# Order of the last two product stages of a block inverse, and of a modulation matmul, in a two-layer diffusion-transformer kernel

## The chip, the cores and the metric

The kernel runs on one core of a Trainium2 chip. The metric is the device time of one execution in microseconds; lower is better. The core has a matmul engine (TensorE, "PE" in the profile, its weight loads "PEld"), VectorE ("DVE"), ScalarE ("ACT"), GpSimd ("POOL"), and a queue of DMA issues ("SP").

## The reference, cut to what matters

One step of a two-layer trunk is computed for 512 latent and 128 context tokens of width 2048. Two pieces of it are touched.

Every layer starts with an RMSNorm that is modulated by a vector computed from the condition:

```python
def adaln(cond, w, b):
    m = (jax.nn.silu(cond) @ w + b)[:, None, :]
    return jnp.split(m, 3, axis=-1)
hp = rmsnorm(xp, norm_g[layer]) * (1.0 + scale_p) + shift_p
```

Layer 1 is a recurrence over tokens, once in each direction, for 32 heads of size 64:

```python
def step(s, inp):
    r_t, w_t, k_t, v_t, kk_t, a_t = inp
    sa = jnp.einsum('bhij,bhj->bhi', s, -kk_t)
    s = s * w_t[:, :, None, :] + sa[..., None] * (kk_t * a_t)[:, :, None, :] + v_t[..., None] * k_t[:, :, None, :]
    return s, jnp.einsum('bhij,bhj->bhi', s, r_t)
```

The kernel does this recurrence in chunks of 64 tokens. In a chunk each step reads what the earlier steps of the chunk wrote, which is a triangular system of 64 x 64 for each head. Its inverse is what the function below builds.

## The kernel before, in words

**The start (lines 244 to 304).** The modulation of layer 0 is a product of a 2048-vector (two of them, padded to 32 columns) with a matrix of 2048 x 6144, of which eight blocks of 512 columns are done here. `adaln` takes one block: for each of 16 slices of the 2048 it loads a tile `araw` of 128 x 512 floats (256 KB, pool `xt0`, eight buffers) and multiplies (line 176). The four column tiles of the array, 32 columns wide, are used in turn (`tile_position=(0, j)`), and their four partial sums are added at the end, after a copy to SBUF (`row`, line 180) and four transposes (line 183). Four rounds `b` of the loop at line 291 do two blocks each. In rounds 1 to 3 the generator is advanced by the numbers in `JW` between six projection jobs of the round before (`part` and `first`, 24 matmuls at line 126 each), and after the blocks `modulate` makes the inputs of the next jobs. A projection loads a tile `raw`, ScalarE makes its rounded part `whi` (line 100), GpSimd the remainder `wlo` (line 101), and three products are added up. All DMAs are issued in order from the SP queue.

**The recurrence (layer 1).** It has 32 units, of a pair of heads and a half of the tokens of both directions. `unit(n)` writes PE's instructions by hand (`manual_schedule`): the steps of the recurrence of unit `n` (`stage_c`), between them steps of `fill`, which put projection matmuls of line 126 there, and then the table `P2`, which prepares the next units: `inv` is `stage_inv`, `bk` transposes (`pbk`, copied to `BKn` by ScalarE), `pre` transposes (`pvt`, copied to `UV`) and products (`pmv`), `bonus` a sum (`pbn`), `a2` Gram products (`gram`, which VectorE masks into `GG`). The other engines' order is made by a scheduler from the program's order and priorities.

`stage_inv` has four stages of 32 x 32 products, all written into one PSUM tile `CC`. The two directions `z` have partitions 0 to 63 and 64 to 127; in each, the 64 x 64 system is split into two blocks of 32, and there are ten systems `q`.

- Stage 1 (L1243) and stage 2 (L1252) go over `q` outside and the four diagonal tiles of the array inside, 40 products each.
- VectorE then transposes the upper blocks (L1257) and ScalarE copies all four blocks of the result to `xd` (L1259).
- Stage 3 (L1265) multiplies by the off-diagonal block of the system, all ten products of the first direction on one tile of the array, (0, 32), then all ten of the second on another, (64, 96). It overwrites the lower blocks in PSUM. ScalarE copies the result (L1268, named `DD`).
- Stage 4 (L1272) does the same on the tiles (32, 0) and (96, 64), and overwrites the upper blocks. ScalarE copies with a minus sign (L1275).

A 32-bit float product is run by the engine as two passes, so 40 products show as 80 records, and 20 as 40.

Of the kernel before, what the change touches and what calls it, by code (L numbers as in the profile page):

```python
# [14 lines left out]
AF = mybir.ActivationFunctionType  # L15
# [6 lines left out]
KT = 16  # L22
# [31 lines left out]
def kernel(  # L54
# [5 lines left out]
    act, dve, pool, pe = nc.scalar, nc.vector, nc.gpsimd, nc.tensor  # L60
# [42 lines left out]
    def sigmoid(out, in_, tmp, scale=-1.0, bias=None, out_scale=-1.0):  # L103
        if bias is None:
            act.activation(out=tmp, in_=in_, func=AF.Exp, scale=scale)
        else:
            act.activation(out=tmp, in_=in_, func=AF.Exp, scale=scale, bias=bias)
        act.activation(out=tmp, in_=tmp, func=AF.Ln, bias=one_b[0:tmp.shape[0]])
        act.activation(out=out, in_=tmp, func=AF.Exp, scale=out_scale)
# [20 lines left out]
    def chunk(g):  # L130
        for end in g:
            if end:
                break

    def project(*args):
        for _ in project_steps(*args):
            pass
# [28 lines left out]
    def ada_raw(layer, n, k, sb, bufs):  # L166
        raw = sb.tile([128, 512], F32, tag="araw", name="araw", bufs=bufs)
        dma(out=raw, in_=mod_w[layer, n, :, k, :])
        return raw

    def adaln(layer, psp, tag, sb, sc, blocks, bufs):
        for n in blocks:
            ps = psp.tile([128, 512], F32, tag=tag, name="ada")
            for k in range(KT):
                j = 32 * (k % 4)
                pe.matmul(ps[j:j + 32, :], sc[:, k, :], ada_raw(layer, n, k, sb, bufs), start=(k < 4),
                          stop=(k >= 12), tile_position=(0, j))
                yield
            row = sb.tile([128, T], F32, tag="tmp", name="row")[:, 0:512]
            act.activation(out=row, in_=ps, func=AF.Copy)  # L180
            pt = psp.tile([128, 512], F32, tag=tag, name="adat")
            for j in range(4):
                pe.transpose(pt[:, j * 128:(j + 1) * 128], row[:, j * 128:(j + 1) * 128], ident)
            ada_end(layer, n, pt.rearrange("p (j g r) -> p j r g", j=4, g=4)[:, :, 0:2, :], 4)
# [57 lines left out]
    pm = l0.enter_context(tc.tile_pool(name="pm", bufs=2, space=PSUM))  # L242

    with tc.tile_pool(name="x0", bufs=1, side="right") as xp0, \
            tc.tile_pool(name="x0t", bufs=2, side="right") as xt0:
        cond = xp0.tile([128, KT, 2], F32, name="cond")
        dma(out=cond, in_=condT)
        sct = xp0.tile([128, KT, 2], F32, name="sct")
        sigmoid(sct, cond, sct)
        dve.tensor_tensor(out=scs, in0=sct, in1=cond, op=ALU.mult)  # L250
        sc = xp0.tile([128, KT, 32], F32, name="sc")
        dve.memset(sc, 0.0)
        dve.tensor_copy(out=sc[:, :, 0:2], in_=scs)
        x0 = xp0.tile([128, KT, T], F32, name="x0")
        pt = pj.tile([128, 1024], F32, tag="pj", name="ss")
        pss = [pt[:, 512 - HT:512], pt[:, 512:512 + HT]]
        for k in range(KT):
            dma(out=x0[:, k, :], in_=xT[k])
            sq = xt0.tile([128, T], F32, tag=("tmp", "hm")[k % 2], name="sq")
            act.activation(out=sq, in_=x0[:, k, :], func=AF.Square)  # L260
            if k % 2:
                dve.tensor_tensor(out=sq, in0=sq, in1=sqe, op=ALU.add)
                for p, (a, b) in zip(pss, HALVES):
                    pe.matmul(p[:, 0:HT], ones, sq[:, a:b], start=(k == 1), stop=(k == KT - 1))
            sqe = sq
        rs0 = xp0.tile([128, T], F32, name="rs0")
        rstd(rs0, pss, 1.0 / 2048, eps_b)
        for k in range(KT):
            dve.tensor_tensor(out=x0[:, k, :], in0=x0[:, k, :], in1=rs0, op=ALU.mult)
        first = [pj.tile([128, 1024], F32, tag="pj", name="first") for _ in range(2)]  # L270
        fg = [project_steps([p[:, 512 - HT:512], p[:, 512:512 + HT]], w_l0[24 + j], KT, 128, h0hi, h0lo, HALVES, 4)
              for j, p in enumerate(first)]

        def half(g):
            for _ in range(6):
                next(g)

        def part(j, b, out):
            p = pS.tile([128, 1024], F32, tag="S", name="part")
            ks = slice(4 * b, 4 * b + 4)  # L280
            project([p[:, 512 - HT:512], p[:, 512:512 + HT]], w_l0[26 + j][:, ks, :], 4, 128,
                    h0hi[:, ks, :], h0lo[:, ks, :], HALVES, 4)
            X, acc = p[:, 512 - HT:512 + HT], accs[j][:, 0:T]
            with tc.high_priority(offset=1500):
                if b == 0:
                    dve.tensor_copy(out=acc, in_=X)
                else:
                    dve.tensor_tensor(out=acc if out is None else out, in0=acc, in1=X, op=ALU.add)

        JOBS, JW = (0, 4, 1, 5, 2, 3), (None, (5, 5, 5, 5, 5, 5), (5, 5, 5, 5, 5, 5), (5, 6, 7, 8, 6, 0))  # L290
        for b in range(4):
            ga = adaln(0, pm, "pm", xt0, sc, (b, 4 + b), 8)
            if b:
                for i, job in enumerate(JOBS):
                    for _ in range(JW[b][i]):
                        next(ga, None)
                    if job < 4:
                        part(job, b - 1, None)
                    else:
                        chunk(fg[job - 4])  # L300
            for _ in ga:
                pass
            for k in range(4 * b, 4 * b + 4):
                modulate(x0[:, k, :], 0, k, h0hi, h0lo, xt0)
        lp = xp0.tile([128, 256], F32, name="lp")
        dma(out=lp, in_=vec[:, NVEC - 256:NVEC])
        lamt = xp0.tile([128, 132], F32, name="lamt")
        dve.tensor_tensor(out=lamt[:, 0:64], in0=lp[:, 0:64], in1=lp[:, 64:128], op=ALU.mult)
        dve.tensor_tensor(out=lamt[:, 64:128], in0=lp[:, 128:192], in1=lp[:, 192:256], op=ALU.mult)
        dve.tensor_reduce(out=lamt[:, 128:130], in_=lamt[:, 0:128].rearrange("p (a b) -> p a b", a=2),  # L310
                          axis=AX.X, op=ALU.add)
        act.activation(out=lamt[:, 128:130], in_=lamt[:, 128:130], func=AF.Exp)
        dve.tensor_tensor(out=lamt[:, 130:131], in0=lamt[:, 129:130], in1=lamt[:, 128:129], op=ALU.subtract)
        nlam = cst.tile([128, 1], F32, name="nlam")
        dve.tensor_scalar(out=nlam, in0=lamt[:, 130:131], scalar1=-LAM_INIT, scalar2=None, op0=ALU.add)
# [522 lines left out]
    with ExitStack() as l1:  # L838
# [32 lines left out]
        for t in Xds:  # L871
            dma(out=t.rearrange("p c -> (p c)").rearrange("(p c) -> p c", p=128),
                in_=xds[0][:, 0:5, :].rearrange("p q t -> p (q t)"))
# [349 lines left out]
        def stage_inv(i, u):  # L1223
            un = units[(i, u)]
            zh = halves_of(u)
            G = un.GAq
            xd = un.xd = xds[u]
            Dn, D = un.DD[:, 0], un.DD[:, 1]
            grp = [(64 * z + 32 * m, 32 * m, 2 * ca) for z, _, _, ca, _ in zh for m in range(2)]
# [5 lines left out]
            def pa(o):  # L1235
                return PA[o:o + 32].rearrange("p b (q t) -> p b q t", t=32)

            def b2(t):
                return t.rearrange("p (b q) t -> p b q t", b=2)
# [10 lines left out]
            for q in range(10):  # L1250
                for o, col, q0 in grp:
                    pe.matmul(blk(o, q), t16[o:o + 32, q, :], D[o:o + 32, q, :],  # L1252
                              start=True, stop=True, tile_position=(o, o))
            xn = un.DD[:, 0]
            for o, col, q0 in grp:
                if col == 0:
                    dve.transpose(out=b2(xn[o:o + 32]), in_=pa(o))  # L1257
            for o, col, q0 in grp:
                act.activation(out=b2(xd[o:o + 32, :, col:col + 32]), in_=pa(o), func=AF.Copy)  # L1259
            yield  # L1260
            t32 = xn
            for z, a, b, ca, cb in zh:
                o = 64 * z
                for q in range(10):
                    pe.matmul(blk(o + 32, q), G[o:o + 32, 2 * ca + q, 32:64], xn[o:o + 32, q, :],  # L1265
                              start=True, stop=True, tile_position=(o, o + 32))
            for o in (0, 64):
                act.activation(out=b2(t32[o + 32:o + 64]), in_=pa(o + 32), func=AF.Copy)  # L1268
            yield
            for o in (0, 64):  # L1270
                for q in range(10):
                    pe.matmul(blk(o, q), t32[o + 32:o + 64, q, :], xd[o + 32:o + 64, q, 32:64],  # L1272
                              start=True, stop=True, tile_position=(o + 32, o))
            for o in (0, 64):
# [418 lines left out]
```

## Time and profile before

| what | value |
|---|---|
| median of 3 runs | 3726.73 us (3720.97 to 3733.14) |
| the profiled execution's own time | 3717.45 us |
| its span, first to last instruction | 3715.7 us |
| PE busy | 3491.8 us, 94% of the span |
| DVE, ACT, POOL busy | 59%, 43%, 32% |
| mean granted clock of PE | 0.98 |

The span covers all but 1.75 us of the execution's own time. Busy time of PE is the time in which a matmul is under way; matmuls overlap, so a busy engine need not be at its best rate.

### The profile page before, as it was taken

Reading aid. Unit: us, or ns where it says so; the run is one execution under the profiler, and the core shown is the slowest. Engines: PE = TensorE matmul, PEld = TensorE weight load, DVE = VectorE, ACT = ScalarE, POOL = GpSimd, SP = SyncE. Lnnn points to the kernel's source line nnn. Section 1 sums busy time; section 2 is a strip of 40 time slices with the busy share of each in tenths; the row PEclk is TensorE's granted clock in tenths of the full one; section 3 lists DMA queues with packets and bytes.
Section 4 is the critical chain, followed back from the end, with each engine's and each line's share of the span. In section 5 each row is a group of like instructions: output and inputs, shape, how many; then the busy total and the mean of one; then the engine's idle time right before and its main releaser. Section 6 shows DMA issues by size and latency. Waiting matters only on the chain. (4 is left out here: it accounts for less than half of the span.)

```text
span 3715.7 us, 83258 instructions
## 1 busy us (share of the span) xinstructions
PE 3491.8 (94%) x34176; PEld 3054.6 (82%) x34176; DVE 2183.1 (59%) x4232; ACT 1608.9 (43%) x3310; POOL 1189.5 (32%) x1094
## 2 busy tenths in 40 slices
PE   7999999999999989999999999999999999999998
PEld 3788889988888889887777787878878878787898
DVE  3355655666667564556666566666666666666402
ACT  2344443444444422544454444444444545445322
POOL 1222112222223344432333332323323333332444
PEclk9999999999999989999999999999999999999999
DMA  8723433333333464322222222222232222223534
GB/s 288 240 80 93 126 100 113 108 102 108 107 108 118 144 204 152 104 77 62 73 62 68 59 65 73 62 65 62 63 76 67 61 67 67 65 68 89 162 101 142
DMA packets 388462, 376.18 MB, mean 101 GB/s; under 512 B 200496, under 2 KB 242416, under 8 KB 388080
## 3 DMA queue, kind: packets, MB, share of 16 engines
q1 hardware_dynamic: 388080, 370.86, 34.3%
q8 instruction: 268, 4.39, 0.5%
q14 instruction: 114, 0.93, 0.1%
HBM read 328.51 MB, written 42.24 MB: 100 GB/s over the span
## 5 line engine op out<-in xcount | busy, mean ns | idle before, releaser
L101 POOL TENSOR_TENSOR wlo<-raw,whi 128x512 fp32r<-128x512 f32 (+1 forms) x628 | 854.4, 1361 | 2032.1 <-PE pj L126 1232.3
L126 PE MATMUL pj<-h0hi,wlo 128*128 128x320 f32 x4448 | 1091.2, 324 | 17.5 <-POOL wlo L101 17.3
L126 PE MATMUL pj<-h0hi,whi 128*128 128x320 f32 x4448 | 1089.2, 324 | 4.8 <-DVE gt L951 3.1
L126 PE MATMUL pj<-h0lo,whi 128*128 128x320 f32 x4448 | 1081.2, 322 | 1.1 <-POOL h0lo L101 0.8
L126 PEld LDWEIGHTS pj<-h0hi,wlo 128*128 128x128 f32 x4448 | 749.6, 192 | 51.9 <-POOL wlo L101 20.7
L126 PEld LDWEIGHTS pj<-h0hi,whi 128*128 128x128 f32 x4448 | 749.2, 192 | 38.3 <-issue 9.1
L126 PEld LDWEIGHTS pj<-h0lo,whi 128*128 128x128 f32 x4448 | 751.8, 191 | 29.2 <-issue 8.0
L100 ACT ACTIVATE whi<-raw 128x512 fp32r<-128x512 f32 (+1 forms) x628 | 390.5, 623 | 734.6 <-PE pj L126 444.0
L198 DVE SCALAR_TENSOR_TENSOR aacc<-araw,scs,aacc 128x512 f32<-128x512 f32 x480 | 401.7, 885 | 20.0 <-DMA araw<-in_dram 19.0
L362 DVE TENSOR_REDUCE nm<-S 128x1 f32<-128x768 f32 (+1 forms) x120 | 98.5, 821 | 257.6 <-PE S L374 257.5
L722 DVE SCALAR_TENSOR_TENSOR x<-pj,mod,xr 128x512 f32<-128x512 f32 (+2 forms) x68 | 33.3, 526 | 251.8 <-PE pj L126 246.1
L365 ACT ACTIVATE P<-S,nm 128x768 f32<-128x768 f32 (+1 forms) x120 | 95.2, 793 | 164.8 <-DVE nm L362 164.3
L1118 DVE TENSOR_TENSOR GG<-gram,con 128x512 f32<-128x512 f32 (+1 forms) x192 | 107.8, 597 | 79.6 <-PE gram L1114 79.5
L1303 ACT ACTIVATE Yn<-CC 128x128 f32<-128x128 f32 x160 | 44.4, 277 | 217.2 <-DVE rhs L1333 209.1
L1114 PE MATMUL gram<-AR,BK 64*128 64x128 f32 x1280 | 115.9, 295 | 20.8 <-DVE GG L1118 13.8
L1114 PEld LDWEIGHTS gram<-AR,BK 64*128 64x128 f32 x1280 | 91.8, 191 | 46.3 <-DVE GG L1118 24.1
L1348 DVE COPY UV<-CC 64x128 f32<-64x128 f32 x160 | 47.1, 295 | 130.6 <-ACT UV L1347 129.2
L1054 PE MATMUL plo<-lr,lw 96*128 96x320 f32 x256 | 104.1, 489 | 6.9 <-DMA lr<-lorad 6.6
L1347 ACT ACTIVATE UV<-CC 64x128 f32<-64x128 f32 x160 | 43.2, 270 | 148.0 <-PE CC L1345 147.4
L564 PE MATMUL po<-PT,vt 128*128 128x128 f32 x800 | 103.2, 276 | 0.1
L564 PEld LDWEIGHTS po<-PT,vt 128*128 128x128 f32 x800 | 98.0, 191 | 4.2 <-issue 2.5
L1056 ACT ACTIVATE tmp<-plo,vecs 128x320 f32<-128x320 f32 x128 | 67.5, 527 | 67.2 <-PE plo L1054 67.2
(338 smaller groups left out, 5306.3 us busy)
## 6 DMA issues: line engine op xcount, KB each, us to landing
raw<-in_dram SPq DMA_DIRECT2D x612, 256.0 KB
araw<-in_dram SPq DMA_DIRECT2D x384, 256.0 KB
lr<-lorad SPq DMA_DIRECT2D x128, 120.0 KB
Ld<-GG SPq DMA_DIRECT2D x64, 160.0 KB
lw<-in_dram SPq DMA_DIRECT2D x128, 48.0 KB
x<-in_dram SPq DMA_DIRECT2D x16, 320.0 KB
xr<-in_dram SPq DMA_DIRECT2D x16, 320.0 KB
DD<-Xd SPq DMA_DIRECT2D x32, 160.0 KB
```

The costliest lines, as they stand in the source:

```text
L100: act.activation(out=hi, in_=src, func=AF.Copy)
L101: (lo_eng or pool).tensor_tensor(out=lo, in0=src, in1=rf(hi), op=ALU.subtract)
L126: pe.matmul(p[:n, 0:b - a], w, x[:, kk ^ flip, a:b], start=(kk == order[0] and i == 0), stop=(kk == order[-1] + kc - 1 and i == 2))
L198: dve.scalar_tensor_tensor(out=acc[:, s], in0=raw, scalar=scs[:, k, s:s + 1], in1=acc[:, s], op0=ALU.mult, op1=ALU.add)
L362: dve.tensor_reduce(out=nm, in_=S[:, 0:nk], axis=AX.X, op=ALU.max, negate=True)
L365: act.activation(out=P[:, 0:nk], in_=S[:, 0:nk], func=AF.Exp, bias=nm, accum_out=l)
L564: pe.matmul(po[:, 0:128], H.vt[:, kt, :], PT[:, j, :], start=(j == 0), stop=(j == n - 1))
L1054: pe.matmul(ps[:, 0:HT], lw, lo, start=True, stop=True)
L1056: act.activation(out=hv(tmp, z, ca, cb), in_=c3(ps[:, 0:HT]), func=AF.Exp, scale=-1.0, bias=nw0[:, bcol:bcol + 1])
L1114: pe.matmul(ps[:, j * 128:(j + 1) * 128], BK[hs, c + j, :, :].rearrange("p a t -> p (a t)"), AR[hs, c + j, :, :].rearrange("p a t -> p (a ...
L1118: dve.tensor_tensor(out=GG[:, c:c + n, h, :], in0=ps[:, 0:n * 128].rearrange("p (j t) -> p j t", t=128), in1=maskg.rearrange("p (o t) -> p ...
L1348: dve.tensor_copy(out=UV[64:128, cgs[1], :], in_=pu[1][64:128])
```

## The change

In `adaln` the four loads of a round of the four column tiles are issued first, then its four products, and the generator stops once a round instead of once a product. It also stops after the copy `row`, so that other work stands before the transposes. `JW` counts in these new steps, and the pool has twelve `araw` buffers. In `stage_inv` stages 3 and 4 go over `q` outside and the two directions inside, so that two tiles of the array take turns. Of the four copies to `xd` only the two of the lower blocks, which stage 3 overwrites, stand ahead of stage 3, and each is written between the transposes; the two of the upper blocks are issued after stage 3's own copies, ahead of stage 4, which overwrites them.

```diff
     def adaln(layer, psp, tag, sb, sc, blocks, bufs):
...
-            for k in range(KT):
-                j = 32 * (k % 4)
-                pe.matmul(ps[j:j + 32, :], sc[:, k, :], ada_raw(layer, n, k, sb, bufs), start=(k < 4),
-                          stop=(k >= 12), tile_position=(0, j))
+            for g in range(0, KT, 4):
+                raws = [ada_raw(layer, n, g + j, sb, bufs) for j in range(4)]
+                for j, raw in enumerate(raws):
+                    pe.matmul(ps[32 * j:32 * j + 32, :], sc[:, g + j, :], raw, start=(g == 0),
+                              stop=(g == KT - 4), tile_position=(0, 32 * j))
                 yield
             row = sb.tile([128, T], F32, tag="tmp", name="row")[:, 0:512]
             act.activation(out=row, in_=ps, func=AF.Copy)
+            yield
...
-        JOBS, JW = (0, 4, 1, 5, 2, 3), (None, (5, 5, 5, 5, 5, 5), (5, 5, 5, 5, 5, 5), (5, 6, 7, 8, 6, 0))
+        JOBS, JW = (0, 4, 1, 5, 2, 3), (None, (2, 1, 2, 2, 1, 2), (2, 1, 2, 2, 1, 2), (2, 2, 1, 2, 3, 0))
         for b in range(4):
-            ga = adaln(0, pm, "pm", xt0, sc, (b, 4 + b), 8)
+            ga = adaln(0, pm, "pm", xt0, sc, (b, 4 + b), 12)
...
             for o, col, q0 in grp:
                 if col == 0:
                     dve.transpose(out=b2(xn[o:o + 32]), in_=pa(o))
-            for o, col, q0 in grp:
-                act.activation(out=b2(xd[o:o + 32, :, col:col + 32]), in_=pa(o), func=AF.Copy)
+                else:
+                    act.activation(out=b2(xd[o:o + 32, :, col:col + 32]), in_=pa(o), func=AF.Copy)
             yield
             t32 = xn
-            for z, a, b, ca, cb in zh:
-                o = 64 * z
-                for q in range(10):
+            for q in range(10):
+                for z, a, b, ca, cb in zh:
+                    o = 64 * z
                     pe.matmul(blk(o + 32, q), G[o:o + 32, 2 * ca + q, 32:64], xn[o:o + 32, q, :],
                               start=True, stop=True, tile_position=(o, o + 32))
             for o in (0, 64):
                 act.activation(out=b2(t32[o + 32:o + 64]), in_=pa(o + 32), func=AF.Copy)
+            for o in (0, 64):
+                act.activation(out=b2(xd[o:o + 32, :, 0:32]), in_=pa(o), func=AF.Copy)
             yield
-            for o in (0, 64):
-                for q in range(10):
+            for q in range(10):
+                for o in (0, 64):
                     pe.matmul(blk(o, q), t32[o + 32:o + 64, q, :], xd[o + 32:o + 64, q, 32:64],
                               start=True, stop=True, tile_position=(o + 32, o))
```

**ScalarE around stages 3 and 4 of the tenth unit, before.** `xd` are the copies of the blocks, `BKn` and `UV` copies for the steps `bk` and `pre`, `DD` the copies of stage 3's result, `whi` the rounding of a projection weight, `hl` a split for `bonus`.

```order
1495 L1259 ACTIVATE xd_14636<-CC 32x10x32 x4
1496 L1183 ACTIVATE BKn<-pbk 128x512
1497 L1205 ACTIVATE UV<-pvt 64x512 x2
1498 L1268 ACTIVATE DD<-CC 32x320 x2
1499 L100 ACTIVATE whi<-raw 128x512
1500 L100 ACTIVATE hl<-kzs 128x320
1501 L1183 ACTIVATE BKn<-pbk 128x256
1502 L1275 ACTIVATE xd_14636<-CC 32x10x32 x2
```

The same place now, where four more lines in the file have moved the numbers (L1261 and L1272 are the copies to `xd`, L1270 is stage 3's result):

```order
1511 L1261 ACTIVATE xd_14636<-CC 32x10x32
1512 L1185 ACTIVATE BKn<-pbk 128x512
1513 L1261 ACTIVATE xd_14636<-CC 32x10x32
1514 L1207 ACTIVATE UV<-pvt 64x512 x2
1515 L100 ACTIVATE whi<-raw 128x512
1516 L1270 ACTIVATE DD<-CC 32x320 x2
1517 L1272 ACTIVATE xd_14636<-CC 32x10x32 x2
1518 L100 ACTIVATE hl<-kzs 128x320
1519 L1185 ACTIVATE BKn<-pbk 128x256
1520 L1279 ACTIVATE xd_14636<-CC 32x10x32 x2
```

Two copies have left the place ahead of `UV`; two stand behind `DD`, and `whi` has moved from behind the `DD` copies to ahead of them. The `whi` has moved so in 12 of the 32 units, and in four others another ScalarE operation has (`gt` or `sqk`). By the semaphores, the second transposition of VectorE now waits for the first of the two copies, and the second copy for that transposition; before, the four copies waited for both transpositions.

**PE in round 1 of the start, before:** the products of the modulation (`ada`) between the jobs, whose own rows are left out but for the first.

```order
8 L176 MATMUL ada<-araw,sc 32x512 x8
9 L126 MATMUL part<-h0hi,whi 128x320 x2
...
21 L176 MATMUL ada<-araw,sc 32x512 x2
...
34 L176 MATMUL ada<-araw,sc 32x512 x5
...
47 L176 MATMUL ada<-araw,sc 32x512
...
51 L183 MATMUL adat<-con,row 128x128 x4
52 L176 MATMUL ada<-araw,sc 32x512 x4
```

And now (line 177 is the product, 185 the transposition):

```order
8 L177 MATMUL ada<-araw,sc 32x512 x8
9 L126 MATMUL part<-h0hi,whi 128x320 x2
...
21 L177 MATMUL ada<-araw,sc 32x512 x4
...
34 L177 MATMUL ada<-araw,sc 32x512 x4
...
47 L185 MATMUL adat<-con,row 128x128 x4
48 L177 MATMUL ada<-araw,sc 32x512 x8
```

Runs of 2, 5 and 1 have become runs of 4 and 4. Over rounds 1 to 3 the 96 products stand in 24 runs before and in 21 now. With four products to a turn of the four column tiles, and a new turn for what is over, the runs make up 36 turns before (12, 11 and 13 by round) and 30 now (8, 11 and 11); in rounds 2 and 3 the scheduler still breaks some turns up (9, 1, 2, 1 and 3 products in round 2).

## Rows read from the trace of the kernel before

**Rows 1.** The page's first part: busy time, share of the span, instructions.

```profile
PE 3491.8 (94%) x34176; PEld 3054.6 (82%) x34176; DVE 2183.1 (59%) x4232; ACT 1608.9 (43%) x3310; POOL 1189.5 (32%) x1094
```

**Rows 2.** Windows: stretch, length, busy us of engines, granted clock, DMA share, GB/s.

```profile
14.00:22.00 8.00, 7.24 (x21) 3.94 (x20) 4.01 (x5) 6.07 (x9) 0.00 (x0) 1.00 1.04 394
22.00:56.00 34.00, 26.62 (x93) 6.01 (x92) 16.02 (x30) 6.89 (x12) 0.00 (x0) 1.00 0.89 302
56.00:162.00 106.00, 102.88 (x608) 69.16 (x608) 21.74 (x45) 26.70 (x45) 27.96 (x22) 1.00 0.77 259
1640.00:3430.00 1790.00, 1678.92 (x22608) 1429.38 (x22608) 1160.39 (x2643) 853.59 (x1880) 567.07 (x630) 0.98 0.26 67
```

**Rows 3.** PE's groups by line, 1640 to 3430 us: busy, mean ns, idle before.

```profile
L1114 PE MATMUL gram<-AR,BK 64*128 64x128 f32 x1240 | 112.9, 295 | 19.5 <-DVE GG L1118 13.8 <-ACT MV L1220 3.6 <-DVE BK L1097 0.6
...
L1272 PE MATMUL CC<-xd,DD 32*32 32x32 f32 x1280 | 46.0, 197 | 0.0
L1265 PE MATMUL CC<-DD,GG 32*32 32x32 f32 x1280 | 44.1, 194 | 27.5 <-ACT xd L1259 27.2
L1252 PE MATMUL CC<-DD,t 32*32 32x32 f32 x2560 | 29.6, 194 | 2.0 <-issue 1.3 <-DVE t L1246 0.4
```

**Rows 4.** Timeline of PE in one unit: start, length us, instructions, idle before.

```profile
2384.95 0.89 PE L1252 MATMUL CC<-DD,t 32*32 32x32 f32 x80
...
2390.45 1.35 PE L1265 MATMUL CC<-DD,GG 32*32 32x32 f32 x40 [1.19 <-ACT xd L1259]
...
2394.18 1.35 PE L1272 MATMUL CC<-xd,DD 32*32 32x32 f32 x40
```

**Rows 5.** Timeline of PE: products of 64 columns on two and on four tiles.

```profile
2413.23 0.45 PE L1345 MATMUL CC<-rhs,xd 64*64 64x64 f32 x8
...
2416.09 0.34 PE L1299 MATMUL CC<-S,AR 64*64 64x64 f32 x8
```

**Rows 6.** Timeline of VectorE in the unit of rows 4.

```profile
2387.50 1.05 DVE L1257 STREAM_TRANSPOSE DD<-CC 32x320 f32<-32x320 f32 x2
2393.19 0.49 DVE L1426 TENSOR_TENSOR vT<-vT,pbn 128x320 f32<-128x320 f32 x1 [4.64 <-PE pbn L1015]
```

**Rows 7.** Timeline of ScalarE in the same unit.

```profile
2388.65 1.75 ACT L1259 ACTIVATE xd<-CC 32x320 f32<-32x320 f32 x4 [3.30 <-DVE DD L1257]
2390.42 0.60 ACT L1183 ACTIVATE BKn<-pbk 128x512 f32<-128x512 f32 x1
2391.04 1.20 ACT L1205 ACTIVATE UV<-pvt 64x512 f32<-64x512 f32 x2
2392.26 0.87 ACT L1268 ACTIVATE DD<-CC 32x320 f32<-32x320 f32 x2
...
2393.59 0.62 ACT L100 ACTIVATE whi<-raw 128x512 fp32r<-128x512 f32 x1
```

**Rows 8.** Waits of the whole span: us in total, times, longest us.

```profile
ACT whi L100 <- PE pj L126: 444.0, 246, 7.4
...
PE CC L1265 <- ACT xd L1259: 27.2, 25, 2.6
```

**Rows 9.** PE's modulation products, 14 to 165 us, by line.

```profile
L176 PE MATMUL ada<-araw,sc 128*32 128x512 f32 x256 | 60.5, 603 | 5.6 <-DMA araw<-in_dram 5.6
```

**Rows 10.** Timeline of PE in round 1 of the start.

```profile
61.41 1.05 PE L176 MATMUL ada<-araw,sc 128*32 128x512 f32 x4
62.39 0.56 PE L126 MATMUL first<-h0hi,whi 128*128 128x320 f32 x2
...
66.10 1.90 PE L176 MATMUL ada<-araw,sc 128*32 128x512 f32 x10
67.94 0.56 PE L126 MATMUL part<-h0hi,whi 128*128 128x320 f32 x2
```

## The prediction, made before the result was known

> **What bounds the kernel now.** I read the page's first part, then windows, then PE's groups by line in the stretch of the recurrence, and last timelines of single places.
>
> PE is busy for 94% of the span and no other engine for more than 59% [rows 1]. In the recurrence, 1640 to 3430 us, it is busy for 1679 of 1790 us, and its clock is granted at 0.98; the DMA engines are used for a quarter [rows 2]. PE's order is fixed there, so its own time and its waits add up, and what is taken off either shortens the stretch unless another engine then makes PE wait at a later place.
>
> The last two stages of the inverse are the odd lines in PE's groups. Stage 2 runs 2560 records in 29.6 us busy; stages 3 and 4 run half as many each in 44.1 and 46.0 us [rows 3]. In one unit that is 0.89 us for 80 records against 1.35 us for 40 [rows 4]. A record lasts about 0.19 us in all three [rows 3], so the difference is the distance between starts: (0.89 - 0.19)/79 = 9 ns where four tiles take turns, (1.35 - 0.19)/39 = 30 ns where one tile is used ten products long. Besides, PE stood idle for 27.5 us ahead of stage 3, of which 27.2 us, in 25 waits, ended with the copies to `xd` [rows 3, 8].
>
> The start is bound differently. From 14 to 22 us the DMA engines move 394 GB/s, from 22 to 56 us 302 GB/s at a share of 0.89, with PE waiting in between; from 56 to 162 us PE is busy for 102.9 of 106 us and the DMA share is 0.77 [rows 2]. There PE is the bound, and the modulation products are part of its time: 60.5 us for 128 products up to 165 us [rows 9].
>
> **The change, part by part.**
>
> *Two tiles in turn.* With four tiles, stage 2 does 80 records as 20 turns of four, (0.89 - 0.19)/20 = 35 ns a turn [rows 4]. One tile does a record in 30 ns. A turn thus costs the same whether one or four tiles are in it, and with two tiles stages 3 and 4 have 20 turns too, so they should last as long as stage 2. The only two-tile case of the trace agrees: products of 64 columns take 0.45 us for 8 records on two tiles and 0.34 us on four [rows 5], where one tile, at twice the 30 ns for twice the columns, would take some 7 x 0.06 + 0.22 = 0.64 us. The gain is 44.1 + 46.0 - 2 x 29.6 = **30.9 us** [rows 3]. Its bounds are 0, if pairs don't overlap, and 39 us, if a turn of two takes one tile's 30 ns: 20 x 0.03 + 0.19 = 0.79 us a stage, 90.1 - 64 x 0.79. A tile can't go faster than it does alone.
>
> The Trainium skill speaks against this. "TensorEngine Tiling (Array Packing)", section Performance Considerations, Instruction Overhead, says that every matmul carries about 60 cycles of overhead, so that a narrow one costs as much as one of 60 columns. Read as a cost in series, that is an estimate of 25 ns a record at 2.4 GHz, 40 records would take 1.0 us however they are ordered, and the gain would be nearly nothing. The trace does not agree with that reading: stage 2's records start 9 ns apart [rows 4].
>
> *The wait ahead of stage 3.* Before, two transpositions (1.05 us) and four copies (1.75 us) run one after the other, and stage 3 starts 0.05 us behind the last copy [rows 4, 6, 7]: 2.9 us from the first transposition. Now a transposition, a copy, the second transposition and the second copy alternate, since each waits for the one ahead: 2 x 0.52 + 2 x 0.43 and four gaps of some 0.07 are 2.2 us, 0.7 us less. The copy `BKn` (0.60 us) that now stands between the two copies fits beside the second transposition. At most 25 x 0.7 = 17.5 us of the 27.2 us come back; the least is 0, where the scheduler puts longer work between the two copies, as it does in some units. Waits average 27.2/25 = 1.1 us, but many are shorter than 0.7. I take **10 us**.
>
> *The wait ahead of stage 4.* The two copies that were taken away now stand behind stage 3's copies, and stage 4 must wait for them. In the unit shown, stage 3 ends at 2391.80, ScalarE is done with `UV` at 2392.24 and with stage 3's copies at 2393.13, and stage 4 starts at 2394.18 [rows 4, 7]: a margin of 1.05 us. Two more copies take 0.87 of it. Where `whi` (0.62 us [rows 7]) now stands ahead too, the margin is 0.44 us short, and PE comes 0.48 us earlier by its shorter stage 3; ScalarE in turn has 0.87 us less to do before. Behind a stage 4 that waits, PE's whole queue waits. The least is 0; the most, 0.8 us in each of 32 units, is 26 us. The 12 units with `whi` ahead at 0.6 us, the others near nothing, make some **8 us** lost.
>
> *What is late next.* The Gram products wait 19.5 us, 13.8 of them for VectorE's `GG` [rows 3]. VectorE's long work on the next unit is released by a PE step between stages 3 and 4 (`pbn`; it sat idle 4.6 us until then [rows 6]). What stage 3 saves moves that release too, but what stage 4 saves, (46.0 - 29.6)/32 = 0.5 us a unit [rows 3], does not: where VectorE is already the later one, PE gets to `gram` earlier and waits longer. I count about 14 units so: **7 us** given back, between 0 and all 16 us of stage 4's gain.
>
> *The start.* A run of two products (4 records) holds PE for 62.39 - 61.41 = 0.98 us, a run of five for 67.94 - 66.10 = 1.84 us [rows 10]: the first turn 0.98, each further 0.86 us. Rounds 1 to 3 had 24 runs with 36 turns, now 21 with 30: 24 x 0.98 + 12 x 0.86 less 21 x 0.98 + 9 x 0.86 is **5.5 us**. In round 0 the order of PE is unchanged and the loads set the pace. Twelve buffers allow four more loads under way; if that lifted 302 to 394 GB/s for 34 us, it would give 34 x (1 - 302/394) = 8 us; if the engines are as good as full at their share of 0.89 [rows 2], nothing. I take **3 us**, nearer to the second. Each projection weight now stands behind four or eight modulation loads in SP's queue instead of three to six, up to 2 MB, which the DMA share of 0.77 after 56 us covers; without that cover a job would start some 2 us late.
>
> *Sum.* 30.9 + 10 - 8 - 7 + 5.5 + 3 = 34.4 us. The profiled execution took 3717.45 us, 9.3 us under the median of the runs; from it the sum gives 3683, from the median 3692.3. I forecast **3692 us** for the median.
>
> **The rivals.**
>
> *More comes through.* ScalarE's copies stay in stage 4's cover, VectorE keeps up, the loads speed up: 30.9 + 17.5 + 5.5 + 8 = 62 us, 3665 us. For it: PE is the bound nearly everywhere. Against it: rows 3 show VectorE late already.
>
> *ScalarE becomes the bound.* Stage 4 waits in every unit: 30.9 + 10 - 26 - 7 + 5.5 = 13 us, 3713 us. For it: a margin of 1.05 us that loses 0.87. The Trainium skill, "TensorEngine Tiling (Array Packing)", PSUM Bottleneck, has it that tiling speeds up the products but not the copies out of PSUM, and that these then bind; by the rows here they bind only in part.
>
> *Turns don't pay.* The pairs don't overlap: 10 - 8 + 5.5 + 3, 10 us, 3716 us. Against it: rows 4 and 5.
>
> *Slower.* A `whi` waits for PE to release its buffer, up to 7.4 us at a time [rows 8]. Now 12 of them stand ahead of the copies that stage 4 waits for. If PE's releasing matmul stands just ahead of stage 4, or GpSimd frees the raw tile late, ScalarE blocks and PE with it. It decides from (34.4 + 8)/12 = 3.5 us a unit; at 7.4 us the kernel takes 3727 - 42 + 89 = 3774 us. Against it: in the unit shown and its like no idle time stands before that `whi` [rows 7].
>
> **Chances.** The forecast (20 to 48 us gained) 0.66, more 0.12, ScalarE bound 0.12, no overlap 0.06, slower 0.04. A measurement of this kernel can tell about 0.3%, 11 us, from no change. Of the ScalarE case two thirds, of the no-overlap case a third lie beyond that: faster 0.66 + 0.12 + 0.08 + 0.02 = 0.88, same 0.08, slower 0.04. The range of eight in ten goes from 3669 (most of the better case left out) to 3714 (ScalarE's case in).
>
> **What would show it.** Stages 3 and 4 at 0.85 to 0.9 us for 40 records; PE's idle time ahead of stage 3 at 15 to 20 us; a new wait ahead of stage 4 of 4 to 12 us, in the units with `whi` ahead; the idle time before `gram` up by 5 to 10 us; the last transposition of the start 5 to 12 us earlier. I am wrong if the stages stay above 1.2 us, or if the new waits on ScalarE and VectorE together exceed 30 us.

## The result, and the profile after

The changed kernel takes 3666.8 us (median of four, 3659.3 to 3670.2) against 3727.7 us for the kernel before beside it: a ratio of 0.985, with an interval of 0.983 to 0.987. By the medians that is 61 us faster, by the ratio 55, where 3692 us (35 us faster) were forecast. Timed again on another occasion the ratio was 0.987 (0.985 to 0.989), 50 us. The profiled execution took 3666.4 us, its span is 3664.6 us: 51.1 us under the span of before.

The page's first part of the changed kernel, against [rows 1]:

```profile
PE 3443.2 (94%) x34176; PEld 3014.7 (82%) x34176; DVE 2190.1 (60%) x4232; ACT 1608.0 (44%) x3310; POOL 1192.0 (33%) x1094
```

PE has 48.6 us less busy time with the same 34,176 instructions, and its weight loads 39.9 us less; the other engines differ by 7 us at most. In sum the gain is in how fast PE's instructions run, hardly in how long it waits. Its groups by line in the recurrence of the changed kernel, 1623 to 3377 us, against [rows 3] (L1267 is stage 3, L1276 stage 4, L1254 stage 2):

```profile
L1116 PE MATMUL gram<-AR,BK 64*128 64x128 f32 x1240 | 117.5, 301 | 24.8 <-DVE GG L1120 14.6 <-ACT MV L1222 8.4 <-DVE BK L1099 0.6
...
L1254 PE MATMUL CC<-DD,t 32*32 32x32 f32 x2560 | 29.7, 194 | 2.0 <-issue 1.4 <-DVE t L1248 0.4
...
L1276 PE MATMUL CC<-xd,DD 32*32 32x32 f32 x1280 | 26.7, 194 | 5.5 <-ACT xd L1272 5.4
L1267 PE MATMUL CC<-DD,GG 32*32 32x32 f32 x1280 | 26.3, 192 | 16.1 <-ACT xd L1261 15.7
```

Stages 3 and 4 fell from 44.1 and 46.0 us to 26.3 and 26.7. The wait ahead of stage 3 fell from 27.5 to 16.1 us, a new one of 5.5 us stands ahead of stage 4, and the Gram products wait 24.8 us for 19.5. Windows of the start, against [rows 2] (same columns):

```profile
14.00:22.00 8.00, 7.04 (x21) 3.15 (x20) 4.00 (x5) 5.62 (x8) 0.00 (x0) 1.00 1.05 393
22.00:56.00 34.00, 29.95 (x123) 9.64 (x121) 17.55 (x30) 9.65 (x16) 4.64 (x4) 1.00 1.05 383
56.00:162.00 106.00, 100.87 (x652) 75.16 (x653) 28.86 (x56) 31.33 (x52) 28.65 (x23) 1.00 0.74 249
```

From 22 to 56 us the loads now run at 383 GB/s for 302. The transpositions that end the start's modulation come at 149.0 us for 161.7.

By stretch the two spans differ so: the start 12.7 us, the untouched code between it and the recurrence (1480.9 to 1474.5 us) 6.4, the recurrence from its first stage 1 to its last stage 4 (1783.8 to 1752.0) 31.8, the rest 0.2. The second profile of the changed kernel gives 10.7, 5.5, 35.4 and 2.0.

### The profile page after: what moved, and what is told of

The parts are those of the page before. It is cut to its first block, busy times and chain, and to the rows that moved or that the text cites. A ratio compares the mean times of both kernels' runs of the same rounds, so it can differ in the third digit from the quotient of the medians.

```text
span 3664.6 us, 83198 instructions
## 1 busy us (share of the span) xinstructions
PE 3443.2 (94%) x34176; PEld 3014.7 (82%) x34176; DVE 2190.1 (60%) x4232; ACT 1608.0 (44%) x3310; POOL 1192.0 (33%) x1094
## 5 line engine op out<-in xcount | busy, mean ns | idle before, releaser
L200 DVE SCALAR_TENSOR_TENSOR aacc<-araw,scs,aacc 128x512 f32<-128x512 f32 x480 | 409.8, 902 | 16.8 <-DMA araw<-in_dram 15.9
L1352 DVE COPY UV<-CC 64x128 f32<-64x128 f32 x160 | 47.1, 294 | 130.2 <-ACT UV L1351 128.7
```

Of the source, the lines that this page charges most:

```text
L200: dve.scalar_tensor_tensor(out=acc[:, s], in0=raw, scalar=scs[:, k, s:s + 1], in1=acc[:, s], op0=ALU.mult, op1=ALU.add)
L1352: dve.tensor_copy(out=UV[64:128, cgs[1], :], in_=pu[1][64:128])
```

## The experiments

Ratios are to the kernel before on the same chip, with 95% intervals; a gain in us behind a ratio is worked out from it. All profiles are of one execution.

**The start alone.** The modulation part of the change (rounds of four, the stop after `row`, `JW`, twelve buffers) on the inverse of before.

> Only the modulation part of the change (turns of four, new step counts, twelve buffers); the inverse as before. Theory: the start gives 13 us by itself, of which 6 to 7 come in round 0 from loads that run at about 385 GB/s instead of 302 between 22 and 56 us, and 6 from fewer turns in rounds 1 to 3; the recurrence keeps its 27.5 us of idle time ahead of stage 3. Ratio 0.9965. Rival: the loads were as good as full, the start gives only the 5.5 us of the turns, and what more the change gained lies in the inverse. Ratio 0.9985.

Measured: 0.997 (0.996 to 0.998), 11 us. The transpositions of the second block come at 43.2 us, the last at 151.5, against 43.0 and 149.0 in the changed kernel (43.1 and 151.0 in its second profile). The theory holds: the start is worth what its trace shows.

**The inverse alone.** The rest of the change, on the start of before.

> Only the inverse's part of the change; the start as before. Theory: stages 3 and 4 take 26 us each instead of 44 and 46, idle time ahead of stage 3 falls from 27.5 to 16 us, stage 4 gets 5 us of it, Gram products some 6 us more: 30 to 35 us gained, ratio 0.991. Rival: the start and the inverse add up to less than the whole change, because a part of the gain was the drift between two profiles: 25 us, ratio 0.9935.

Measured: 0.991 (0.990 to 0.993), 32 us. Stages 26.6 and 27.4 us busy, idle ahead of them 17.3 and 5.8 us, ahead of `gram` 23.3: as the theory had it.

**The order of the products alone.** In stages 3 and 4 the loops are exchanged; the copies stay as before.

```diff
-            for z, a, b, ca, cb in zh:
-                o = 64 * z
-                for q in range(10):
+            for q in range(10):
+                for z, a, b, ca, cb in zh:
+                    o = 64 * z
```

> Only the order of the products in stages 3 and 4; all four copies stay ahead of stage 3. Theory: the order gives most of the inverse's gain: 37 us less PE time, idle time ahead of stage 3 stays at 27 to 30 us, none ahead of stage 4, 4 to 8 us more ahead of the Gram products: 28 to 33 us gained, ratio 0.992. Rival: without the copies moved, PE only waits longer for ScalarE and VectorE, so that under 15 us are left, ratio 0.996.

Measured: 0.994 (0.992 to 0.995), 24 us, although the stages fell to 26.2 and 27.0 us busy. `gram` in the recurrence of this kernel:

```profile
L1114 PE MATMUL gram<-AR,BK 64*128 64x128 f32 x1240 | 117.0, 298 | 29.9 <-ACT MV L1220 14.2 <-DVE GG L1118 14.2 <-DVE BK L1097 0.6
```

It waits 29.9 us for 19.5: 10 of the 37 us are given back there at once. The gain is less than the theory's, more than the rival's.

**The copies alone.** Only the two copies of the lower blocks ahead of stage 3, the other two behind stage 3's own.

> Only the copies moved; stages 3 and 4 keep their order on one tile at a time. Theory: idle time ahead of stage 3 falls to about 16 us, ahead of stage 4 under 2 us appear since stage 3 is still long: 8 to 11 us gained, ratio 0.9975. Rival: the copies are the greater part of the gain, because the wait ahead of stage 3 is on the chain from unit to unit: 20 us or more, ratio 0.9945.

Measured: 0.996 (0.994 to 0.997), 16 us. Idle ahead of stage 3 is 20.1 us, ahead of stage 4 0.9. Neither side: the theory's 0.9975 lies outside of the interval and its 16 us of idle time weren't reached, and the rival's 0.9945 lies just inside it, its 20 us above what was measured. The wait fell by 7.4 us only, and the time by twice that; what else there is goes with the clock, of which below.

**The buffers alone,** 12 for 8 in the start of before.

> The kernel before with nothing changed but the number of `araw` buffers, 12 for 8. Theory: in round 0 the loads set the pace and what they lack is requests under way, so that the buffers alone bring the whole gain there: from 22 to 56 us some 380 GB/s for 302, the transpositions of the second block of round 0 at 43 us for 49.4, the last transposition of the start near 155 us for 161.7, and the time 6 to 7 us shorter (ratio 0.998). Rival: the gain came from the four loads being issued together, and buffers alone change nothing: second transposition at 49 us, last one at 161, ratio 1.000.

Measured: 0.998 (0.997 to 0.999), 7 us. From 22 to 56 us 358 GB/s, second transpositions at 45.0 us, last at 156.1 (161.7 before; 159.5 to 163.1 in five other kernels with the start untouched). The theory holds in the main: the buffers alone bring the greater part of what round 0 gains, though not the 380 GB/s and 43 us that it expected; the changed kernel has these with the rounds as well.

**The rounds alone,** with eight buffers.

> The new order of the modulation (rounds of four, the new JW, the stop after row), but 8 buffers as before. Theory: round 0 stays as it was (second block's transpositions at 49 us), and rounds 1 to 3 give the 5.5 us that were worked out from the turns: the last transposition near 156 us for 161.7, ratio 0.9985. Rival: issuing four loads together is what speeds round 0 up: second block's transpositions at 43 us, the last one near 149, and the ratio of the whole start part, 0.997.

Measured: 1.000 (0.999 to 1.001); last transposition at 163.0 us. Neither side: the rounds alone give nothing. The trace says why. In round 1 of this kernel, a timeline of PE:

```profile
71.16 2.27 PE L177 MATMUL ada<-araw,sc 128*32 128x512 f32 x14
73.94 1.05 PE L177 MATMUL ada<-araw,sc 128*32 128x512 f32 x2 [0.51 <-DMA araw<-in_dram]
```

and the same run of eight products in the changed kernel:

```profile
64.77 1.92 PE L177 MATMUL ada<-araw,sc 128*32 128x512 f32 x16
66.62 0.56 PE L126 MATMUL first<-h0hi,whi 128*128 128x320 f32 x2
```

With eight buffers the longer run catches up with its loads and holds PE from 71.16 to 74.91 us, with twelve from 64.77 to 66.62. Over rounds 1 to 3 the modulation's runs hold PE, from their first start to the next other product, for 43.2 us before, 43.1 with rounds alone, 39.4 with buffers alone and 37.0 with both.

**The changed kernel again.**

> The changed kernel again, on the same chip as the kernels beside it. The start alone had given 11 us and the inverse alone 32, 43 together, where the changed kernel had given 51 by the two profiles and 61 by the medians. Theory: the parts add up, and what is over was the drift of the granted clock between executions: ratio 0.9865 to 0.988 (45 to 50 us). Rival: the parts help each other (a shorter start leaves the rest in another state): 0.9845 or lower again, with the recurrence shorter than the 1753 us that the inverse alone had.

Measured: 0.987 (0.985 to 0.989), 50 us; recurrence 1748.4 us, start to 151.0. Start and inverse alone make 43 us, so the parts add up within these intervals, and the theory's ratio holds; the rival's 0.9845 lies just outside.

**Stage 3 alone and stage 4 alone** in turns of two, the rest as before.

> The kernel before with the two directions in turn in stage 3 alone. Stage 3 falls to 26 us busy (17 to 18 less), the rest of the code as before. Theory: what stage 3 saves moves the step `pbn` that releases VectorE too, so the Gram products wait hardly longer (19.5 to at most 22 us idle) and 14 to 18 us come through, ratio 0.995 to 0.9965. Rival: what is saved anywhere in the unit is given back at the Gram products alike: idle there 24 to 25 us, half of what both stages together gave, 12 us, ratio 0.997.

> The kernel before with the two directions in turn in stage 4 alone. Stage 4 falls from 46 to 27 us busy, 19 less. Theory: it stands behind the step that releases VectorE, so that PE only gets to the Gram products earlier: idle there 27 us or more (8 more than before), pmv 2 more, and 8 to 11 us come through, ratio 0.997 to 0.998. Rival: as for stage 3, idle 24 to 25 us and 12 us or more come through, the two kernels alike within 3 us.

Measured: stage 3 alone 0.994 (0.992 to 0.996), 22 us, nearly as much as both together (24); stage 4 alone 1.001 (1.000 to 1.003), nothing, and rather a loss. The groups of the recurrence with stage 3 in turns:

```profile
L1114 PE MATMUL gram<-AR,BK 64*128 64x128 f32 x1240 | 113.2, 294 | 23.2 <-DVE GG L1118 14.7 <-ACT MV L1220 6.5 <-DVE BK L1097 0.6
...
L1272 PE MATMUL CC<-xd,DD 32*32 32x32 f32 x1280 | 43.9, 194 | 0.0
...
L1265 PE MATMUL CC<-DD,GG 32*32 32x32 f32 x1280 | 26.7, 193 | 27.1 <-ACT xd L1259 26.8
```

and with stage 4 in turns:

```profile
L1114 PE MATMUL gram<-AR,BK 64*128 64x128 f32 x1240 | 116.2, 298 | 29.4 <-DVE GG L1118 16.2 <-ACT MV L1220 11.7 <-DVE BK L1097 0.6
...
L1265 PE MATMUL CC<-DD,GG 32*32 32x32 f32 x1280 | 44.9, 195 | 25.4 <-ACT xd L1259 25.1
...
L1272 PE MATMUL CC<-xd,DD 32*32 32x32 f32 x1280 | 27.8, 197 | 0.0
```

Each stage saves some 18 us of PE. Of stage 4's, 9.9 us come back as idle time at `gram`, of stage 3's 3.7; by all of PE's idle time in the recurrence (table below) it is 12.6 and 8.5, a smaller difference. The theory's direction holds. Its size fails for stage 4, where 8 to 11 us were expected and the interval ends before 2; for stage 3 it isn't settled (14 to 18 expected, 13 to 30 by the interval), and `gram` waits 23.2 us for at most 22. What is missing for stage 4 is the clock.

**Where the clock was low.** In the trace of before PE is granted 1.2 GHz (0.50) for short stretches instead of 2.4. One of them, in windows of the fifteenth unit of before (columns as in [rows 2], the granted clock is the one ahead of the DMA share), and PE's stage 3 there:

```profile
2436.00:2447.00 11.00, 11.00 (x234) 9.71 (x234) 8.26 (x14) 5.36 (x9) 6.23 (x7) 1.00 0.26 63
2449.40:2456.00 6.60, 6.27 (x59) 5.83 (x60) 1.22 (x4) 3.99 (x9) 0.06 (x1) 0.50 0.00 0
```

```profile
2449.73 2.15 PE L1265 MATMUL CC<-DD,GG 32*32 32x32 f32 x40 [2.60 <-ACT xd L1259]
```

PE waits 2.60 us, then runs stage 3 on one tile after the other in 2.15 us instead of 1.35. By the trace's clock records the stretch begins at 2449.3 us, 0.4 us ahead of stage 3. The same unit of the changed kernel, where the wait is shorter:

```profile
2417.70:2424.00 6.30, 6.26 (x111) 5.91 (x112) 3.78 (x6) 6.18 (x14) 1.35 (x1) 1.00 0.13 38
```

```profile
2417.74 0.82 PE L1267 MATMUL CC<-DD,GG 32*32 32x32 f32 x40 [0.81 <-ACT xd L1261]
```

The ninth unit shows the two orders behind the same wait. Before, the clock falls behind stage 3, and stage 4 takes 2.15 us:

```profile
2105.75 1.35 PE L1265 MATMUL CC<-DD,GG 32*32 32x32 f32 x40 [2.58 <-ACT xd L1259]
...
2109.64 2.15 PE L1272 MATMUL CC<-xd,DD 32*32 32x32 f32 x40
```

```profile
2108.00:2114.80 6.80, 6.80 (x60) 6.32 (x59) 3.92 (x9) 3.14 (x8) 2.04 (x2) 0.50 0.01 2
```

With stage 3 alone in turns it stays at full speed:

```profile
2107.21 0.82 PE L1265 MATMUL CC<-DD,GG 32*32 32x32 f32 x40 [2.59 <-ACT xd L1259]
...
2109.93 1.35 PE L1272 MATMUL CC<-xd,DD 32*32 32x32 f32 x40
```

```profile
2108.10:2114.80 6.70, 6.68 (x92) 6.17 (x93) 5.11 (x8) 4.67 (x11) 2.89 (x3) 1.00 0.03 6
```

The table adds up these stretches over the recurrence, by the traces' clock records; each is put down to the longest idle time of PE shortly ahead of it, and the last two columns are parts of the one before.

| kernel | recurrence, us | PE idle | at 1.2 GHz | behind stage 3's wait | behind `gram`'s |
|---|---|---|---|---|---|
| before | 1783.8 | 111.0 | 71.7 | 47.8 | 13.7 |
| start alone | 1789.1 | 111.2 | 78.5 | 44.4 | 17.1 |
| buffers alone | 1792.2 | 112.2 | 85.3 | 51.2 | 13.7 |
| rounds alone | 1788.6 | 108.4 | 88.7 | 64.9 | 13.7 |
| copies alone | 1770.0 | 104.9 | 54.6 | 30.7 | 13.7 |
| stage 4 alone | 1792.8 | 123.6 | 99.0 | 47.8 | 34.1 |
| stage 3 alone | 1766.5 | 119.5 | 47.8 | 17.1 | 13.7 |
| order alone | 1755.3 | 126.7 | 41.0 | 10.2 | 23.9 |
| inverse alone | 1752.8 | 111.3 | 75.1 | 23.9 | 20.5 |
| changed | 1752.0 | 113.3 | 68.3 | 13.7 | 23.9 |
| changed, again | 1748.4 | 114.4 | 54.6 | 13.7 | 23.9 |

The first four have the same inverse and show the spread. With stage 3 on one tile and the copies as before, 44 to 65 us at 1.2 GHz stand behind its wait; with turns of two, 10 to 24. The wait itself is no shorter in "stage 3 alone" and "order alone" (27.1 and 26.4 us), so what PE runs behind it matters, not the wait alone. The single waits say where this holds. Of 44 waits of 0.8 to 1.6 us in the five kernels with one tile and the copies as before, 26 had a stretch at 1.2 GHz begin at them or right behind; with turns of two in stage 3 it was 1 of 18 (two kernels), and 2 of 24 where the copies are moved too (six). Of the waits of 1.6 us or more it was 26 of 27, 4 of 12, and 15 of 17: behind the longest waits the clock still falls in the changed kernel, and behind the fifteenth unit's it does in "stage 3 alone" too.

At 1.2 GHz the records of the projections start 267 ns apart instead of 147 (medians of before), so that nearly half of the time is lost; what follows takes it as half, as an estimate. In all, against the 71.7 to 88.7 us of the first four, stage 3 alone has 47.8, which gains it 12 to 20 us on top of 17.4 saved and 3.7 given back (part of it is in the 17.4 already). Stage 4 alone has 99.0, since the stretches behind `gram`, whose wait has grown, have doubled: 5 to 14 us lost, which with the 12.6 us of idle time eats up its 18. Against the profile of before the sums come out near: 17.4 + 12.0 - 8.5 = 20.9 us for stage 3 alone, whose recurrence is 17.3 shorter, and 18.2 - 13.7 - 12.6 = -8.1 for stage 4 alone, whose recurrence is 9.0 longer.

The timed runs say the same without the choice of one execution. Their mean granted clock over the whole program is 0.979 to 0.980 before (three occasions, 15 to 23 runs each) and 0.979 in the three kernels that change the start alone; it is 0.983 for stage 3 alone (6 runs) and for the copies alone (5), 0.984 for the order alone (5), and 0.977 for stage 4 alone (11). If the time goes as the granted clock, stage 3 alone gains an estimated 12 us by it (0.9830 against 0.9798) and stage 4 alone loses 9 (0.9774).

**The copies of the lower blocks ahead of both transpositions,** in the changed kernel.

```diff
             for o, col, q0 in grp:
-                if col == 0:
-                    dve.transpose(out=b2(xn[o:o + 32]), in_=pa(o))
-                else:
+                if col:
                     act.activation(out=b2(xd[o:o + 32, :, col:col + 32]), in_=pa(o), func=AF.Copy)
+            for o, col, q0 in grp:
+                if col == 0:
+                    dve.transpose(out=b2(xn[o:o + 32]), in_=pa(o))
```

> The changed kernel, with the two copies of the lower blocks ahead of both transpositions in the program, in place of each between them. Theory: the chain from stage 2 to stage 3 is the sum of the same two copies and two transpositions, 2 x 0.52 + 2 x 0.43 us and the gaps, whatever their order, so the idle time ahead of stage 3 stays at 14 to 17 us (it now ends with VectorE) and the time within 0.2% of the changed kernel's. Rival: alternating costs two more hand-overs between the engines and lets BKn and whi of ScalarE in between; without them idle ahead of stage 3 falls below 10 us and the time by 6 to 10 us more.

> The kernel with the copies of the lower blocks ahead of both transpositions once more, on another occasion: its ratio of 0.9828 lay 0.0038 under that of the changed kernel beside it, with few runs of either. Theory: idle time ahead of stage 3 again at 11 to 13 us, and the time at 0.982 to 0.985 of the kernel before. Rival: the difference was the granted clock of that occasion: 0.9855 or more, with the same idle times.

Measured: 0.983 (0.981 to 0.985), and again 0.985 (0.982 to 0.987). The interval of the first just reaches that of the changed kernel beside it, that of the second overlaps it: by the ratios 14 and 7 us better than the changed kernel timed again, 9 and 3 than its first timing, not settled. The theory of the first run fails: the order of the copies does change the chain, though not to the rival's 10 us of idle time. Of the second run the theory's idle time came again, but its interval takes in the rival's 0.9855. Idle ahead of stage 3 is 11.8 and 11.5 us for 16.1 and 15.2, in the stages' other times nothing changes, and at 1.2 GHz there are 34.1 and 37.5 us (51.2 with the same inverse in the next kernel). The ninth unit shows the shorter chain. ScalarE in the changed kernel, where `hl` and `BKn` come between the two copies:

```profile
2078.24 0.43 ACT L1261 ACTIVATE xd<-CC 32x320 f32<-32x320 f32 x1
2078.69 0.47 ACT L100 ACTIVATE hl<-sqk 128x320 fp32r<-128x320 f32 x1
2079.18 0.60 ACT L1185 ACTIVATE BKn<-pbk 128x512 f32<-128x512 f32 x1
2079.80 0.43 ACT L1261 ACTIVATE xd<-CC 32x320 f32<-32x320 f32 x1
```

ScalarE and VectorE here:

```profile
2074.37 0.83 ACT L1024 ACTIVATE sqk<-kT,vecs 128x640 f32<-128x640 f32 x1 [3.35 <-DVE AR L1092]
2075.23 0.87 ACT L1259 ACTIVATE xd<-CC 32x320 f32<-32x320 f32 x2
```

```profile
2076.13 1.03 DVE L1262 STREAM_TRANSPOSE DD<-CC 32x320 f32<-32x320 f32 x2 [1.88 <-ACT xd L1259]
```

The first transposition of the changed kernel starts at 2076.67 us, its last copy ends at 2080.23: 3.6 us; here first copy to last transposition take 1.9. Both start late, for VectorE is at `AR` until then, and `sqk`, ahead of the copies here, waits for that: this part of the wait stays.

**The same with 16 buffers.**

> The same with 16 `araw` buffers for 12. Theory: in round 0 the DMA engines are full with 12 (383 GB/s of the 394 seen at the start), so nothing is left to gain there; in rounds 1 to 3 the runs of 16 to 18 records that still hold PE for 2.9 to 3.9 us instead of 1.85 wait for loads, and four more buffers bring back at most 3 to 4 us: last transposition of the start at 147 to 151 us, time as the kernel beside it within 0.1%. Rival: more buffers let the modulation's loads push the projections' weights back: the waits for `whi` in the start (2.8 us) grow by more than that and the last transposition is later than 152 us.

Measured: 0.984 (0.981 to 0.986), 3663.4 us beside 3666.9 with twelve. The last transposition comes at 145.5 us for 149.8, a little more than the theory's 3 to 4 us earlier and ahead of its 147 to 151, and the runs of the modulation hold PE for 34.0 us for 37.2. The loads of round 0 gain hardly (384 GB/s for 376), as the theory had it. The time can't tell it.

## Why the prediction was right, and where it was off

The direction and the main mechanism were right, the size was short. 3666.8 us stand 2 us under the range of 3669 to 3714; by the two ratios to the 3726.7 us from which the forecast started it would be 3672 and 3677. The 50 to 61 us gained lie beyond the 20 to 48 that had the greatest chance.

Gains in us, by the two profiles of the changed kernel against the one of before:

| step | predicted | measured |
|---|---|---|
| stages 3 and 4 in turns of two | 30.9 | 37.1, 37.0 |
| wait ahead of stage 3 | 10 | 11.4, 12.3 |
| new wait ahead of stage 4 | -8 | -5.5, -6.1 |
| `gram` waits longer | -7 | -5.3, -5.8 |
| all else in the recurrence | 0 | -5.9, -2.0 |
| start, rounds 1 to 3 | 5.5 | 6.3, 4.4 |
| start, loads of round 0 | 3 | 6.4, 6.3 |
| code that isn't touched | 0 | 6.6, 7.5 |
| sum | 34.4 | 51.1, 53.6 |

*Turns of two: the mechanism right, the size too small.* A stage now lasts 0.82 us, (0.82 - 0.19)/20 = 32 ns a turn: nearer to one tile's 30 ns than to the 35 of four that were assumed, and the gain nearer to its upper bound of 39. At full clock the stages' first to last start went from 1.16 to 0.63 us, 64 x 0.53 = 34 us; the other 3 us are stages that ran at 1.2 GHz before, most of them stage 4 (2.7 us over its full speed before, 0.4 after). By the rule of the Trainium skill that spoke against it ("TensorEngine Tiling (Array Packing)", Instruction Overhead), read in series, 40 records would still need an estimated 1.0 us; in the 0.82 us they start 16 ns apart where that reading has 25, so it does not hold for two tiles either.

*The waits on ScalarE: right in size, not in where.* Ahead of stage 4 the profile after shows the new wait that was forecast. ScalarE and PE in the nineteenth unit, where `sqk` has come ahead:

```profile
2640.32 1.20 ACT L1207 ACTIVATE UV<-pvt 64x512 f32<-64x512 f32 x2
2641.42 0.82 ACT L1024 ACTIVATE sqk<-kT,vecs 128x640 f32<-128x640 f32 x1
2642.26 0.87 ACT L1270 ACTIVATE DD<-CC 32x320 f32<-32x320 f32 x2
2643.14 0.86 ACT L1272 ACTIVATE xd<-CC 32x320 f32<-32x320 f32 x2
```

```profile
2644.06 0.82 PE L1276 MATMUL CC<-xd,DD 32*32 32x32 f32 x40 [0.72 <-ACT xd L1272]
```

Twelve such waits make 5.4 us, the longest 1.0. But the 12 units with `whi` ahead, to which the prediction gave 0.6 us each, have only 1.5 us of them; the longer ones stand behind `sqk` (1.9 us in three units) and `hl` (1.0 in one), and 0.8 us with nothing moved ahead. No `whi` ahead of the copies held ScalarE for the 3.5 us of the slower rival, and the waits are far from the 26 us of ScalarE as the bound. The section of the Trainium skill that stood for that last rival ("TensorEngine Tiling (Array Packing)", PSUM Bottleneck) says that after a speedup of the products the copies may become the bottleneck; here they took back 5.5 of 37 us.

*What is late next: the direction right.* That stage 4's saving is given back at `gram` and stage 3's mostly not was the step's reasoning, and the two stages alone show it there, 9.9 against 3.7 us; by all of PE's idle time, 12.6 against 8.5, the two are less far apart. That `gram` lost less in the whole change than with the order alone (5.3 against 10.4) fits the new wait ahead of stage 4, if what PE loses there it doesn't wait for later; no run shows this by itself. The two terms were summed as if they were independent.

*The start: two sizes, one cause wrong.* Round 0 took most of its upper bound, 6.4 of 8 us: a DMA share of 0.89 was read as good as full, and in the changed kernel it is 1.05 (1.01 with the buffers alone). In five other kernels with the start untouched the second transpositions come at 47.1 to 49.3 us for the 49.4 of before, so that some 4 to 6 us are the change's. For rounds 1 to 3 the 5.5 us came out near, but by luck, not by the count of turns that was given: the same 30 turns with eight buffers give nothing, and of the 6.2 us less for which the runs hold PE, twelve buffers alone give 3.8. The row of the trace that was multiplied, 0.86 us a further turn, holds only while the loads are there.

*No term for the clock.* The sum let all time outside the edits stand. Stage 3's order and its shorter wait took away 34 us of the stretches behind that wait (47.8 to 13.7), but others came behind `gram` and elsewhere, so that the recurrence of the changed kernel has 68.3 and 54.6 us at 1.2 GHz where the four with the inverse of before have 81 on average: an estimated 6 to 13 us gained. In the untouched code there were 77.1 us before and 63.4 after, which at half speed is 6.9 us, all of that row of the table; but the other kernels spread over 1477 to 1488 us between start and recurrence, and the two with the copies ahead, which have the same start and code, take 1478.8 and 1483.4, so no effect of the change is shown there.

Of the 17 us between 34.4 and 51.1, the turns brought 6, the start 4, the three waits together 6, the untouched code 7, and the rest of the recurrence took 6. The last 10 us of the 61 are the profile of before, which stood 9 to 10 us under its median, as the prediction said; the repeat gave 50. The time fits the rival by which more comes through (3665 us), but of its reasons only the faster loads held; there is a wait ahead of stage 4 and a longer one at `gram`.

Open stays why the granted clock falls less often behind the same wait when stage 3 runs on two tiles (the stage is also 0.53 us shorter then, and no run separates the two), why it still fell behind nearly all the longest waits once the copies were moved, and whether the copies ahead of both transpositions beat the changed kernel by more than the timings can tell.

## What to carry to other kernels

Here a record of a narrow product took 30 ns on one tile used again and again, and two on two tiles took 32 together; where independent systems are at hand, look for such turns first. Read a saving by what stands behind it: the same 18 us of PE time gave 22 us in one stage and nothing in the next. A part of that is the wait at the engine that is late next (3.7 us longer for the one, 9.9 for the other); the greater part goes with the granted clock, which rose with the one (47.8 us at 1.2 GHz in the recurrence) and fell with the other (99.0). Here longer runs of products needed more loads under way: buffers alone gave 7 us, the longer runs alone nothing, both 11.

## What was not expected of the hardware

- A turn of 32 x 32 products takes 30 ns with one tile, 32 with two and 35 with four, in fp32 at 2.4 GHz.
- All stretches at 1.2 GHz in the recurrence stood close behind an idle time of PE of 0.76 us or more, though most such idle times brought none (15 stretches, 50 idle times in the kernel before). With much the same idle time ahead of stage 3 (25 to 28 us in all) they came to 44 to 65 us where it then ran on one tile and to 10 to 17 us where it ran on two, the copies being as before.
- Eight loads of 256 KB under way gave 302 to 329 GB/s (seven kernels), twelve 358 to 383 (six), sixteen 384, in the same 34 us.
